# Four gate and up pairs of each swiglu FFN in seven half-size products, and the FFN's inner tiles in four groups

## Chip, cores, metric

The kernel runs on one core of a Trainium2 chip, in one launch. The metric is device time in microseconds, the median of several executions. Engines are named as the profile names them: PE is TensorE's matmul, PEld its weight load, DVE VectorE, ACT ScalarE, POOL GpSimd, and SP issues the weight loads from memory.

## What is computed

Two layers of a first block (FFN, mixer, FFN, gated embedding) and one layer of a second block, on 512 tokens of width 1024. The change touches only the swiglu FFNs of the first block, of which there are four (two layers, two FFNs each, hidden width 2816):

```python
def swiglu(x, w_gate, w_up, w_down):
    return (jax.nn.silu(x @ w_gate) * (x @ w_up)) @ w_down

for i in range(DEPTH):                      # DEPTH = 2
    h = rmsnorm(x, g_ffn1_pre[i])
    x = x + 0.5 * rmsnorm(swiglu(h, w1_gate[i], w1_up[i], w1_down[i]), g_ffn1_post[i])
    ...                                     # mixer: projections, two attentions, a convolution
    h = rmsnorm(x, g_ffn2_pre[i])
    x = x + 0.5 * rmsnorm(swiglu(h, w2_gate[i], w2_up[i], w2_down[i]), g_ffn2_post[i])
    ...                                     # gated embedding ("ple")
```

## The kernel before

Activations lie transposed: 128 features on the partitions, 512 tokens along the free axis. A tile is 128 x 512 in float32. Every product is done in three matmuls (`mm3`, L285 to L287): each operand is split into a high part, rounded to the fast float32 format, and a low part, the rest; the products high x high, low x high and high x low are added up in one PSUM bank, and low x low is left out. PSUM has eight banks of 128 x 512 in float32.

**Weights.** A unit is the weights of one output tile: for gate and up, 8 blocks of 128 x 128 (one for each 128 of the 1024 input features). SP loads units into `raw` tiles (L231); `prep` makes `wh` with a cast on ACT (L146) and puts the subtraction that makes `wl` on DVE (L147) into a list, which is flushed at the end of a step. `run` keeps `wu` units prepared ahead of the one in use.

**Order.** Nothing is rescheduled: each engine runs its instructions in the order in which the code of the steps issues them. A step is a matmul group or an evacuation; `later` holds what an evacuation postpones to the next step.

**A swiglu FFN** has 22 inner tiles n. For each, the gate product (8 x 3 matmuls of 512 columns into a bank `gu`) is multiplied on DVE by the token's norm factor `rb` into `gr` (L681) and put through Silu on ACT (L683); the up product likewise into `ur` (L706), then one step later `ur` is multiplied by `gr` (L712), and `split` makes `dh` on ACT (L306) and `dl` on DVE (L307). `pieces = (6, 8, 8)` groups the inner tiles: after each group the down products of that group run, 8 output tiles m, each summing over the group's tiles into a bank `pt`; they are added to `f` (copied on ACT for the first group, added on DVE, L779, for the others).

**The boundary** to the next stage is written out by hand in `PLAN`. The last four output tiles (m = 4 to 7) of the last group, the tail, are computed in two halves of 256 tokens, PA and PB. All four PA halves come first, then the PB halves, each cut in two (`mm_part`). Between the PB pieces stands the chain of the norm over PA: the sum of squares `acc` (L653 on ACT, L655 on POOL or DVE), a transpose on PE (`ss`, L314), a reduction on DVE (L315), the power on POOL (L323), a broadcast on PE (`bc`, L330), a copy on ACT (`sb`, L523), then for each of 8 feature tiles the update on DVE (L538, L539) and the new operand `hh` on ACT (L540), which the next stage's first products (`hd`, L638) read. Between the second FFN of a layer and the embedding stage eight small products (`pp`) stand between tail and head as well.

**The rope tables** (`rope_tables`, L403 to L447) are some thirty DVE instructions for the mixer's angles, hooked into the first FFN.

Of the kernel before, what the change touches and what calls it, by code (L numbers as in the profile page):

```python
# [21 lines left out]
N_ACT = 81  # L22
N_RAW = 4
RAW = 1024
WU_TAIL, WU_SB, WU_MLA = 10, 6, 6
N_TAIL = 4

# [41 lines left out]
class Column:  # L69


    def __init__(self, units, c):
        self.hi = lambda k: units[k].hi(0)[:, c]
        self.lo = lambda k: units[k].lo(0)[:, c]


class Raw:
# [18 lines left out]
class Builder:  # L96
# [31 lines left out]
    def cols_units(self, w, k0, kn, c0, ncol, width=P):  # L128
# [5 lines left out]

        return [Unit(lambda inp, c=c: host(inp, c), (kn, width)) for c in range(c0, c0 + ncol, width)]

    def prep(self, u):

        kn, w = u.dims
# [59 lines left out]
    def run(self):  # L199
# [7 lines left out]
                last[id(u)] = i  # L207
        raws = []
        for u in order:
            if len(raws) < 3 or raws[-1].n + u.n > RAW:  # L210
                raws.append(Raw())
            u.raw, u.at = raws[-1], raws[-1].n
            u.raw.units.append(u)
            u.raw.n += u.n
        for r in raws:
            r.left = sum(-(-u.dims[0] // (T // u.dims[1])) for u in r.units)
        self.declare(raws)
        frees = {}
        for u in order:
# [17 lines left out]
        def flush_low(us=None):  # L237
            keep = []
            for u, f in self.low:
                if us is None or u in us:  # L240
                    f()
                    u.raw.left -= 1
                    if u.raw.left == 0:
                        self.rlive -= 1
                else:
                    keep.append((u, f))
            self.low[:] = keep
            load_raws()

        def prep_next():  # L250
            u = order[self.uptr]
            if u.raw.tile is None:
                flush_low()
            assert u.raw.tile is not None
            self.prep(u)
            self.uptr += 1
            self.live += 1

        pos = {id(u): i for i, u in enumerate(order)}
        for m in range(3):  # L260
# [394 lines left out]
        eng.tensor_tensor(sub.acc[:, t0:t1], sub.acc[:, t0:t1], sq[:, t0:t1], op=ALU.add)  # L655


    def ffn(self, cols, pre, post, wg, wu, uoff, wd, pieces, pmul, padd, conv=None, nxt=None, first=False):
        V, S, G = self.V, self.S, self.G
        HT = sum(pieces)  # L660
        ahead = nxt.ahead if nxt else None
# [56 lines left out]
        def item(n, which):  # L718
            it = Sub()
            it.units = [gu[n] if which == 0 else uu[n]]  # L720

            def mm(p):
                pend[n, which] = self.ps("gu")
                self.mmk(pend[n, which], it.units[0], sub.h, p)

            def evac(p):
                (act_up if which else act_gate)(n, p, pend.pop((n, which)))

            it.mm, it.evac = mm, evac
            return it  # L730
# [8 lines left out]
            head = [Column(sub.by_k, slice(i * P, (i + 1) * P)) for i in range(4)]  # L739
        self.plain_head(sub, head, evac)  # L740

        def body():
            n0 = 0
            early = set()
            for pc, kn in enumerate(pieces):
                final = pc == len(pieces) - 1
# [2 lines left out]
                for n in range(max(n0, 2), n0 + kn, 2):  # L749
                    if final and ahead and n == n0 + kn - 4:  # L750
                        self.step(ahead[1])
                    if n not in early:
                        self.two(item(n, 0), item(n + 1, 0))
                    for i in (n, n + 1):
                        self.both(item(i, 1))
                if not final:
                    for i in (n0 + kn, n0 + kn + 1):
                        early.add(i)
                        self.both(item(i, 0))
                du = self.cols_units(wd, n0, kn, 0, D)  # L760
                for m in range(KD):
                    it = Sub()
# [1049 lines left out]
    def program(self):  # L1812
# [9 lines left out]
        for L in range(2):  # L1822
            ple = self.ple(L, colsA[L])
            c = colsA[L]
            seq.append(
                self.ffn(c, "g_ffn1_pre", "g_ffn1_post", mat("w1_gate", L), mat("w1_up", L), 0, mat("w1_down", L), (6, 8, 8), 4.0 / D, 4.0 * EPS, first=L == 0)
            )
            seq.append(self.mix1(L, c))
            seq.append(
                self.ffn(  # L1830
                    c, "g_ffn2_pre", "g_ffn2_post", mat("w2_gate", L), mat("w2_up", L), 0, mat("w2_down", L), (6, 8, 8), 4.0 / D, 4.0 * EPS, nxt=ple
                )
            )
            seq.append(ple)
# [46 lines left out]
def mat(name, L):  # L1881
    return lambda inp: inp[name][L]
# [28 lines left out]
```

## Time and profile before

| | us |
|---|---|
| median of 3 runs (2872.05 to 2875.48) | 2874.39 |
| the profiled execution | 2872.68 |
| its span, first to last instruction | 2870.8 |
| PE busy in the span | 2846.9 |
| DVE busy | 1706.1 |
| ACT busy | 1250.2 |

The span is what the views show; 1.9 us of the profiled execution lie around it. A matmul's end is modelled by the profile and runs over the start of the next one, so the pace of a row of matmuls is read from their starts, not from the duration of one.

### The profile page before, as it was taken

Reading aid. Unit: us, or ns where it says so; the run is one execution under the profiler, and the core shown is the slowest. Engines: PE = TensorE matmul, PEld = TensorE weight load, DVE = VectorE, ACT = ScalarE, POOL = GpSimd, SP = SyncE. Lnnn points to the kernel's source line nnn. Section 1 sums busy time; section 2 is a strip of 40 time slices with the busy share of each in tenths; the row PEclk is TensorE's granted clock in tenths of the full one; section 3 lists DMA queues with packets and bytes.
Section 4 is the critical chain, followed back from the end, with each engine's and each line's share of the span. In section 5 each row is a group of like instructions: output and inputs, shape, how many; then the busy total and the mean of one; then the engine's idle time right before and its main releaser. Section 6 shows DMA issues by size and latency. Waiting matters only on the chain.

```text
span 2870.8 us, 38496 instructions
## 1 busy us (share of the span) xinstructions
PE 2846.9 (99%) x14942; PEld 2445.0 (85%) x14946; DVE 1706.1 (59%) x3048; ACT 1250.2 (44%) x2464; POOL 217.3 (8%) x252
## 2 busy tenths in 40 slices
PE   9999999999999999999999999999999999999999
PEld 8888898798888998888987898888988889888888
DVE  6454476865434595434668674444788746735458
ACT  5342347653322464322457553323546635433234
POOL 0000110010000220000111100000300001000013
PEclk9999999999999999999999999999999999999999
DMA  5333311123223223222121223233222332322320
GB/s 180 113 103 96 101 64 53 52 82 118 96 96 110 74 77 122 100 91 100 64 83 56 85 74 115 91 103 103 76 81 92 103 103 84 115 96 96 110 96 30
DMA packets 77750, 264.30 MB, mean 92 GB/s; under 512 B 9088, under 2 KB 11008, under 8 KB 77568
## 3 DMA queue, kind: packets, MB, share of 16 engines
q1 hardware_dynamic: 75600, 259.29, 27.0%
q0 software_dynamic: 1536, 2.10, 0.3%
q8 instruction: 118, 1.93, 0.3%
q14 instruction: 64, 0.52, 0.1%
q10 hardware_dynamic: 432, 0.45, 0.0%
HBM read 257.61 MB, written 2.10 MB: 90 GB/s over the span
## 4 chain that ended last, share of the span: by engine, by line
PE 88%; DVE 7%; ACT 4%; issue 1%; DMA 0%; POOL 0%; SPq 0%; ACTq 0%; DVEq 0%
PE gu L286 13%; PE gu L287 13%; PE gu L285 13%; PE hd L638 9%; PE pt L286 8%; PE pt L287 8%; PE pt L285 8%; PE in L285 3%; PE in L286 3%; PE in L287 3%; ACT p L1392 1%; DVE wl L147 1%; DVE ptl L307 1%; DVE p L1401 1%; PE ro L285 1%
## 5 line engine op out<-in xcount | busy, mean ns | idle before, releaser
L147 DVE TENSOR_TENSOR wl<-raw,wh 128x512 fp32r<-128x512 f32 (+1 forms) x993 | 643.7, 693 | 147.7 <-ACT wh L146 143.7
L285 PE MATMUL gu<-hh,wh 128*128 128x512 f32 x1632 | 635.9, 390 | 0.0
L286 PE MATMUL gu<-hl,wh 128*128 128x512 f32 x1632 | 635.0, 389 | 0.0
L287 PE MATMUL gu<-hh,wl 128*128 128x512 f32 x1632 | 635.0, 389 | 0.0
L146 ACT CAST wh<-raw 128x512 fp32r<-128x512 f32 (+1 forms) x993 | 545.1, 605 | 200.0 <-PE pt L286 94.0
L285 PE MATMUL pt<-dh,wh 128*128 128x512 f32 (+1 forms) x1056 | 377.7, 358 | 0.0
L286 PE MATMUL pt<-dl,wh 128*128 128x512 f32 (+1 forms) x1056 | 376.9, 357 | 0.0
L287 PE MATMUL pt<-dh,wl 128*128 128x512 f32 (+1 forms) x1056 | 376.8, 357 | 0.0
L287 PEld LDWEIGHTS gu<-hh,wl 128*128 128x128 f32 x1632 | 306.3, 188 | 63.6
L285 PEld LDWEIGHTS gu<-hh,wh 128*128 128x128 f32 x1632 | 306.4, 188 | 63.4
L286 PEld LDWEIGHTS gu<-hl,wh 128*128 128x128 f32 x1632 | 306.4, 188 | 63.2
L306 ACT CAST dh<-ur 128x512 fp32r<-128x512 f32 x112 | 69.5, 621 | 462.8 <-DVE ur L712 462.8
L655 POOL TENSOR_TENSOR acc<-acc,sq 128x256 f32<-128x256 f32 (+1 forms) x96 | 100.5, 1046 | 1913.0 <-ACT sq L653 1912.3
L286 PEld LDWEIGHTS pt<-dl,wh 128*128 128x128 f32 x1056 | 199.5, 189 | 28.9
L285 PEld LDWEIGHTS pt<-dh,wh 128*128 128x128 f32 x1056 | 199.5, 189 | 28.9
L287 PEld LDWEIGHTS pt<-dh,wl 128*128 128x128 f32 x1056 | 199.5, 189 | 28.6
L706 DVE TENSOR_TENSOR ur<-gu,rb 128x512 f32<-128x512 f32 x102 | 70.4, 690 | 253.2 <-PE gu L287 253.2
L779 DVE TENSOR_TENSOR f<-pt,f 128x512 f32<-128x512 f32 (+1 forms) x100 | 58.4, 584 | 237.4 <-PE pt L287 237.3
L285 PE MATMUL in<-hh,wh 128*128 128x512 f32 x432 | 170.7, 395 | 3.0 <-DVE ptl L307 2.4
L638 PE MATMUL hd<-hh,wh 128*128 128x256 f32 (+1 forms) x672 | 169.8, 291 | 0.3 <-ACT hh L464 0.3
L287 PE MATMUL in<-hh,wl 128*128 128x512 f32 x432 | 168.4, 390 | 0.0
L286 PE MATMUL in<-hl,wh 128*128 128x512 f32 x432 | 168.3, 390 | 0.0
(396 smaller groups left out, 4439.8 us busy)
## 6 DMA issues: line engine op xcount, KB each, us to landing
raw<-in_w_dram SPq DMA_DIRECT2D x449, 512.0 KB, 3.3
raw<-in_w_dram SPq DMA_DIRECT2D x36, 384.0 KB, 3.0
x<-in_x_dram SPq DMA_DIRECT2D x8, 256.0 KB, 6.8
raw<-in_w_dram SPq DMA_DIRECT2D x4, 432.0 KB, 3.4
pt<-in_p_dram SPq DMA_DIRECT2D x6, 256.0 KB, 4.0
out_dram<-pgt SPq DMA_DIRECT2D x10, 128.0 KB, 1.7
qh<-qrh POOLq DMA_DIRECT2D x16, 64.0 KB, 2.1
ql<-qrl POOLq DMA_DIRECT2D x16, 64.0 KB, 2.3
```

The source lines that it names most:

```text
L146: self.S.copy(h, src)
L147: self.low.append((u, lambda h=h, l=l, src=src: self.V.tensor_sub(l, src, h.bitcast(F32))))
L285: self.E.matmul(o, lh, rh, start=start, stop=False, **kw)
L286: self.E.matmul(o, lh, rl, start=False, stop=False, **kw)
L287: self.E.matmul(o, ll, rh, start=False, stop=stop, **kw)
L306: self.S.copy(hi, src)
L307: self.V.tensor_sub(lo, src, hi.bitcast(F32))
L638: self.E.matmul(q, w, h, start=k == 0 and j == 0, stop=k == KD - 1 and j == 2)
L655: eng.tensor_tensor(sub.acc[:, t0:t1], sub.acc[:, t0:t1], sq[:, t0:t1], op=ALU.add)
L706: V.tensor_mul(ur[:, t0:t1], ou, sub.rb[:, t0:t1])
L779: V.tensor_tensor(f, q, f, op=ALU.add)
L1392: S.activation(s.p[t][:, c : c + n], s.sc[t][:, c : c + n], AF.Exp, bias=mx[qb], accum_out=s.sum[:, qb : qb + 1])
```

## The change

In each swiglu FFN the inner tiles n = 9, 11, 15 and 17 take the gate and up products by Strassen's identity. Gate and up weights of one tile are taken as one 2 x 2 matrix of blocks (gate and up, by lower and upper 512 input features) and the tokens as two halves A and B. Instead of 48 matmuls of 512 columns there are seven products of 4 x 3 matmuls of 256 columns, 84 in all, on sums of weight blocks (`part_sums`, tiles `q`) and sums of operand halves (`token_sums`, tiles `ts`, made once per FFN). Their results are put together on DVE and ACT out of two banks, `st.r` and `st.r3`; both halves of `st.r` are used. These tiles stand in turns with plain ones: the steps of tile 9 lie between those of 8, of 11 between those of 10, and so on. While they run, 5 units are prepared ahead instead of 8. The groups of inner tiles become (6, 6, 6, 4). The second block's FFN stays as it is.

```diff
-WU_TAIL, WU_SB, WU_MLA = 10, 6, 6
+WU_TAIL, WU_SB, WU_MLA, WU_SEVEN = 10, 6, 6, 5
+SEVEN = (9, 11, 15, 17)
...
+    def part_sums(self, u):
...
+        def add(key, a, b):
+            q[key] = self.a("q")
+            self.V.tensor_add(q[key], a, b)
+
+        if u.j == 0:
+            add("q1", w["21"], w["22"])
+        elif u.j == 1:
+            add("q2", q.pop("q1"), w["11"])
+        elif u.j == 2:
+            add("q4", q.pop("q2"), w["12"])
+            add("q3", w["11"], w["21"])
...
+        def token_sums(k):
+            g1, g2, x1, x2 = sub.gpre(k), sub.gpre(k + 4), self.X[k], self.X[k + 4]
+            xg, a, b = self.a("xg"), self.a("ta"), self.a("tb")
+            S.activation(xg, x1, AF.Copy, scale=g1)
+            V.tensor_sub(a[:, A], xg[:, A], xg[:, B])
+            V.scalar_tensor_tensor(a[:, B], x2[:, B], g2, xg[:, B], op0=ALU.mult, op1=ALU.subtract)
+            V.scalar_tensor_tensor(b[:, A], x2[:, B], g2, a[:, A], op0=ALU.mult, op1=ALU.add)
+            V.scalar_tensor_tensor(b[:, B], x2[:, A], g2, b[:, A], op0=ALU.mult, op1=ALU.subtract)
+            ah, al, bh, bl = (self.a("ts", F32R) for _ in range(4))
+            self.split(a, ah, al)
+            S.activation(bh, b, AF.Copy, scale=-1.0)
+            V.scalar_tensor_tensor(bl, b, -1.0, bh.bitcast(F32), op0=ALU.mult, op1=ALU.subtract)
...
+        def product(o, part, block, key, start):
+            h, l = part.blocks[block]
+            for k in range(4):
+                c = slice(k * P, (k + 1) * P)
+                self.mm3(o, h[:, c], l[:, c], *operand(key, k), start and k == 0, k == 3, skip=True)
...
+            def one():
+                st.r, st.r3 = self.ps("gu"), self.ps("gu")
+                product(st.r[:, A], u[0], "11", "11", True)
+                product(st.r[:, B], u[0], "q1", "t1", False)
+            def copy():
+                st.s = self.a("s15")
+                S.copy(st.s, st.r)
+            def two():
+                st.s2 = self.a("s2")
+                S.copy(st.s2[:, A], st.r[:, A])
+            def gate_a():
+                V.tensor_tensor(pair(n)[0][:, A], st.r3[:, A], st.s[:, A], op=ALU.add)
+            def gate_b():
+                gr = pair(n)[0]
+                V.tensor_tensor(gr[:, B], st.r[:, B], st.s2[:, A], op=ALU.add)
+                V.tensor_mul(gr, gr, sub.rb)
+                S.activation(gr, gr, AF.Silu)
+                self.later.append(lambda: V.tensor_mul(gr, gr, sub.rb))
+            def up_b():
+                V.scalar_tensor_tensor(pair(n)[1][:, B], st.r[:, A], -1.0, st.s[:, B], op0=ALU.mult, op1=ALU.subtract)
+            def out():
+                gr, ur = raw.pop(n)
+                V.scalar_tensor_tensor(ur[:, A], st.r[:, A], -1.0, gr[:, A], op0=ALU.mult, op1=ALU.mult)
+                V.tensor_mul(ur[:, B], ur[:, B], gr[:, B])
+                hid[n] = (self.a("dh", F32R), self.a("dl", F32R))
+                self.split(ur, *hid[n])
+            def last():
+                step(lambda: product(st.r[:, A], u[3], "22", "t4", False), [u[3]])
+                step(out)
+            step(one, [u[0]])
+            step(copy)
+            if prev:
+                prev()
+            self.both(item(m, 0))
+            step(lambda: product(st.r3[:, A], u[1], "12", "21", True), [u[1]])
+            step(gate_a)
+            step(lambda: product(st.r[:, A], u[1], "q2", "t2", False), [u[1]])
+            step(two)
+            self.both(item(m, 1))
+            step(lambda: product(st.r[:, A], u[2], "q3", "t3", False), [u[2]])
+            step(up_b)
+            step(lambda: product(st.r[:, B], u[2], "q4", "22", False), [u[2]])
+            step(gate_b)
+            return last
...
-mat("w1_down", L), (6, 8, 8), 4.0 / D, 4.0 * EPS, first=L == 0)
+mat("w1_down", L), (6, 6, 6, 4), 4.0 / D, 4.0 * EPS, first=L == 0, seven=SEVEN)
```

Three places in the order of instructions follow. In rows of the order a name with "waits" behind it waits for that engine's counter.

DVE before, in a plain pair of the first FFN: `ur<-gu` is the evacuation of an up product, `wl` a weight's low part, `dl` the low part of the finished inner tile.

```order
L706 TENSOR_TENSOR ur_1492<-gu_1503,rb_483 128x512
L147 TENSOR_TENSOR wl_1529<-raw_1366,wh_1528 128x512
L147 TENSOR_TENSOR wl_1532<-raw_1366,wh_1531 128x512
L712 TENSOR_TENSOR ur_1492<-ur_1492,gr_1491 128x512
L307 TENSOR_TENSOR dl_1535<-ur_1492,dh_1534 128x512
L706 TENSOR_TENSOR ur_1500<-gu_1544,rb_483 128x512
```

DVE now, at tile 17 of the first FFN (with 16 in turns): the same five, then `up_b`, which reads the left half of `st.r` (`gu_2347`).

```order
L775 TENSOR_TENSOR ur_2442<-gu_2487,rb_483 128x512
L200 TENSOR_TENSOR wl_2513<-raw_2383,wh_2512 128x512
L200 TENSOR_TENSOR wl_2516<-raw_2383,wh_2515 128x256
L781 TENSOR_TENSOR ur_2442<-ur_2442,gr_2441 128x512
L376 TENSOR_TENSOR dl_2519<-ur_2442,dh_2518 128x512
L890 SCALAR_TENSOR_TENSOR ur_2461<-gu_2347,s_493_2379 128x256
L884 TENSOR_TENSOR gr_2460<-gu_2347,s_514_2481 128x256
```

PE now, at the same place: the end of the product q3 into the left half of `gu_2347`, then the first matmul of the product q4, into the right half, with a wait on DVE's counter; before, the row of matmuls of the next product stood there without a wait.

```order
L354 MATMUL gu_2347<-ts_805,wh_2376 128x256
L355 MATMUL gu_2347<-ts_806,wh_2376 128x256
L356 MATMUL gu_2347<-ts_805,wl_2377 128x256
L354 MATMUL gu_2347<-hh_244,wh_2373 128x256 [waits DVE_49]
L355 MATMUL gu_2347<-hl_245,wh_2373 128x256
```

The value of the counter is that of `up_b`, in all 16 tiles of this kind.

ACT now, at tile 9 of the first FFN: `s<-gu` is the copy of `st.r`, which PE's fourth product (q2) waits for; it stands behind the two Sin of the rope tables, which wait for DVE.

```order
L514 ACTIVATE rope_s<-ang_1248 128x512 [waits DVE_49]
L515 ACTIVATE rope_c<-rc_1266 128x512 [waits DVE_49]
L375 CAST dh_1289<-ur_884 128x512 [waits DVE_49,PE_49]
L183 CAST wh_1321<-raw_1133 128x512 [waits DMAHW6_49]
L183 CAST wh_1324<-q_1242 128x512 [waits PE_49]
L872 COPY s_287_1327<-gu_1295 128x512 [waits PE_49]
```

Before, Silu and casts stood behind those two, and no copy of a bank that a product waits for.

PE now, in the first output tile of the last group of inner tiles: four groups of three matmuls, one for each inner tile 18 to 21; before there were eight, for 14 to 21.

```order
L354 MATMUL pt_3145<-dh_2951,wh_2948 128x512 [waits Activation_49]
L355 MATMUL pt_3145<-dl_2952,wh_2948 128x512 [waits DVE_49]
L356 MATMUL pt_3145<-dh_2951,wl_2949 128x512
L354 MATMUL pt_3145<-dh_2992,wh_2948 128x512 [waits Activation_49]
L355 MATMUL pt_3145<-dl_2993,wh_2948 128x512 [waits DVE_49]
L356 MATMUL pt_3145<-dh_2992,wl_2949 128x512
L354 MATMUL pt_3145<-dh_3101,wh_2948 128x512 [waits Activation_49]
L355 MATMUL pt_3145<-dl_3102,wh_2948 128x512 [waits DVE_49]
L356 MATMUL pt_3145<-dh_3101,wl_2949 128x512
L354 MATMUL pt_3145<-dh_3136,wh_2948 128x512 [waits Activation_49]
L355 MATMUL pt_3145<-dl_3137,wh_2948 128x512 [waits DVE_49]
```

The last group, of the inner tile finished last (21), now stands fourth instead of eighth.

## Rows read from the trace of the kernel before

**Rows 1.** The page: busy time of each engine; then the chain's shares by engine.

```profile
PE 2846.9 (99%) x14942; PEld 2445.0 (85%) x14946; DVE 1706.1 (59%) x3048; ACT 1250.2 (44%) x2464; POOL 217.3 (8%) x252
PE 88%; DVE 7%; ACT 4%; issue 1%; DMA 0%; POOL 0%; SPq 0%; ACTq 0%; DVEq 0%
```

**Rows 2.** Windows over the first FFN: busy time of each engine, clock, DMA share, GB/s.

```profile
59.00:343.00 284.00, 284.00 (x1255) 235.16 (x1254) 139.81 (x237) 92.84 (x168) 3.77 (x7) 1.00 0.32 102
```

**Rows 3.** Timeline of PE, plain gate products, 96 matmuls apart: start, duration, line.

```profile
59.65 0.39 PE L285 MATMUL gu<-hh,wh 128*128 128x512 f32 x1
...
81.41 0.39 PE L285 MATMUL gu<-hh,wh 128*128 128x512 f32 x1
```

**Rows 4.** Timeline of PE, tail in halves, 25 matmuls of 256 columns apart.

```profile
366.16 0.28 PE L285 MATMUL pt<-dh,wh 128*128 128x256 f32 x1
...
369.16 0.28 PE L286 MATMUL pt<-dl,wh 128*128 128x256 f32 x1
```

**Rows 5.** Timelines of PE, DVE and ACT behind an up product of the second FFN.

```profile
759.96 0.39 PE L285 MATMUL gu<-hh,wh 128*128 128x512 f32 x1
```

**Rows 6.** The same place on DVE: evacuation, weights, product, low part.

```profile
760.16 0.69 DVE L706 TENSOR_TENSOR ur<-gu,rb 128x512 f32<-128x512 f32 x1 [4.75 <-PE gu L287]
760.77 1.29 DVE L147 TENSOR_TENSOR wl<-raw,wh 128x512 fp32r<-128x512 f32 x2
761.97 0.69 DVE L712 TENSOR_TENSOR ur<-ur,gr 128x512 f32<-128x512 f32 x1
763.40 0.69 DVE L307 TENSOR_TENSOR dl<-ur,dh 128x512 fp32r<-128x512 f32 x1 [0.74 <-ACT dh L306]
```

**Rows 7.** The same place on ACT.

```profile
762.75 0.62 ACT L306 CAST dh<-ur 128x512 fp32r<-128x512 f32 x1 [5.64 <-DVE ur L712]
```

**Rows 8.** DVE behind an up product with no weights in between (first FFN).

```profile
123.09 0.69 DVE L706 TENSOR_TENSOR ur<-gu,rb 128x512 f32<-128x512 f32 x1 [3.01 <-PE gu L287]
...
125.19 0.69 DVE L307 TENSOR_TENSOR dl<-ur,dh 128x512 fp32r<-128x512 f32 x1 [0.69 <-ACT dh L306]
```

**Rows 9.** Groups by line and form, DVE: count, busy, mean ns.

```profile
L147 DVE TENSOR_TENSOR wl<-raw,wh 128x256 fp32r<-128x256 f32 x36 | 15.1, 420 | 0.0
```

**Rows 10.** Timelines in the mixer: DVE's low part, and PE, which waits for it.

```profile
576.44 0.69 DVE L307 TENSOR_TENSOR yl<-cv,yh 128x512 fp32r<-128x512 f32 x1
577.18 0.50 PE L286 MATMUL part<-yl,wh 128*128 128x512 f32 x1 [1.25 <-DVE yl L307]
```

**Rows 11.** Boundary behind the first FFN, PE: first PB piece, transpose, broadcast.

```profile
357.44 0.28 PE L285 MATMUL pt<-dh,wh 128*128 128x256 f32 x1
...
360.32 0.38 PE L314 MATMUL ss<-ident,acc 128*128 128x128 f32 x2
...
364.86 0.38 PE L330 MATMUL bc<-ident,s 128*128 128x128 f32 x2
```

**Rows 12.** The same boundary, DVE: sum of squares, weights, reduction, first update.

```profile
358.62 0.42 DVE L655 TENSOR_TENSOR acc<-acc,sq 128x256 f32<-128x256 f32 x1 [0.55 <-ACT sq L653]
...
360.87 1.28 DVE L147 TENSOR_TENSOR wl<-raw,wh 128x512 fp32r<-128x512 f32 x2
362.06 0.42 DVE L315 TENSOR_REDUCE ss<-ss 128x2 f32<-128x256 f32 x1
...
365.68 0.49 DVE L538 SCALAR_TENSOR_TENSOR t<-f,cols,sb 128x256 f32<-128x256 f32 x1 [0.43 <-ACT sb L523]
```

**Rows 13.** The same boundary: POOL's power.

```profile
362.86 0.71 POOL L323 TENSOR_TENSOR s<-ss,mhalf 128x2 f32<-128x2 f32 x1
```

**Rows 14.** ACT's operand of feature tile 5 there.

```profile
373.50 0.51 ACT L540 ACTIVATE hh<-x,cols 128x256 fp32r<-128x256 f32 x1 [1.77 <-DVE x L539]
```

**Rows 15.** DVE at the rope tables: the evacuation ahead, their start, what follows them.

```profile
128.53 0.69 DVE L706 TENSOR_TENSOR ur<-gu,rb 128x512 f32<-128x512 f32 x1 [1.44 <-PE gu L287]
...
134.03 0.43 DVE L410 CAST ang<-pos_i 128x512 f32<-128x512 int32 x1 [1.44 <-DMA pos_i<-in_positions_dram]
...
151.01 1.29 DVE L147 TENSOR_TENSOR wl<-raw,wh 128x512 fp32r<-128x512 f32 x2
```

More of the change, by code (lines that the diff above doesn't have):

```diff
@@ L74, in __init__, with blocks @@
         self.lo = lambda k: units[k].lo(0)[:, c]
+class Quad:
+    def __init__(self, hosts):
+        self.hosts, self.raws, self.q = hosts, None, {}
+        self.parts = [Part(self, j) for j in range(4)]
+    def blocks(self):
+        a, b = (r.tile for r in self.raws)
+        return {"22": a[:, 0:T], "11": a[:, T:], "12": b[:, 0:T], "21": b[:, T:]}
+class Part:
+    n, dims = 1024, (8, P)
+    def __init__(self, quad, j):
+        self.quad, self.j, self.blocks, self.summed = quad, j, {}, False
 class Raw:
@@ L209, in run @@
         for u in order:
+            if isinstance(u, Part):
+                if u.quad.raws is None:
+                    u.quad.raws = [Raw(), Raw()]
+                    for r, host in zip(u.quad.raws, u.quad.hosts):
+                        block = Unit(host, (8, P))
+                        block.at, r.units, r.n = 0, [block], RAW
+                    raws.extend(u.quad.raws)
+                u.raw = u.quad.raws[1]
+                continue
             if len(raws) < 3 or raws[-1].n + u.n > RAW:
@@ L216, in run @@
             r.left = sum(-(-u.dims[0] // (T // u.dims[1])) for u in r.units)
+        for u in order:
+            if isinstance(u, Part):
+                u.quad.raws[0].left, u.quad.raws[1].left = 7, 6
         self.declare(raws)
@@ L241, in flush_low @@
                     f()
[L242 to L244 removed]
+                    for r in (u.quad.raws[: 2 if u.j < 3 else 1] if isinstance(u, Part) else [u.raw]):
+                        r.left -= 1
+                        if r.left == 0:
+                            self.rlive -= 1
                 else:
@@ L257, in prep_next @@
             self.live += 1
+            nxt = order[self.uptr] if self.uptr < len(order) else None
+            if isinstance(nxt, Part) and all(r.tile is not None for r in nxt.quad.raws):
+                self.part_sums(nxt)
         pos = {id(u): i for i, u in enumerate(order)}
@@ L655, in final_sq, with ffn @@
         eng.tensor_tensor(sub.acc[:, t0:t1], sub.acc[:, t0:t1], sq[:, t0:t1], op=ALU.add)
-    def ffn(self, cols, pre, post, wg, wu, uoff, wd, pieces, pmul, padd, conv=None, nxt=None, first=False):
+    def ffn(self, cols, pre, post, wg, wu, uoff, wd, pieces, pmul, padd, conv=None, nxt=None, first=False, seven=()):
         V, S, G = self.V, self.S, self.G
@@ new lines, in operand @@
+        def operand(key, k):
+            if key in ("11", "21", "22"):
+                hh, hl = sub.h[k + 4 * (key[0] == "2")]
+                c = A if key[1] == "1" else B
+            else:
+                i = 0 if key in ("t1", "t3") else 2
+                hh, hl = sums[k][i : i + 2]
+                c = A if key in ("t1", "t2") else B
+            return hh[:, c], hl[:, c]
+        def product(o, part, block, key, start):
[3 more added lines that the diff above has]
+                self.mm3(o, h[:, c], l[:, c], *operand(key, k), start and k == 0, k == 3, skip=True)
@@ L742, in body @@
         def body():
-            n0 = 0
+            n0, left = 0, None
             early = set()
@@ L751, in body @@
                         self.step(ahead[1])
+                    if seven and n == 4:
+                        wu, self.wu = self.wu, WU_SEVEN
+                    if seven and n > seven[-1]:
+                        self.wu = wu
+                    if n + 1 in seven:
+                        left = seven_pair(n, n + 1, left)
+                        continue
                     if n not in early:
@@ L755, in body @@
                         self.both(item(i, 1))
+                        if seven and pc == 0:
+                            self.step(lambda k=i - 2: token_sums(k))
                 if not final:
```

41 lines of the change are left out of this document (39 added, 2 removed).

## The prediction

> **What bounds the kernel now.** I read the page first: PE is busy for 99% of the span and makes up 88% of the chain that ended last [rows 1]. Then the first FFN by itself: PE has work in all of its 284 us, at the full granted clock, while DVE is busy for 139.8 us of them, about half [rows 2]. So in the FFNs a matmul taken away is time gained, as long as PE does not start to wait for something; DVE and ACT cost nothing as long as they keep ahead. The reader is to see two things there: PE's pace, and how far DVE runs behind PE when it evacuates a bank. The pace: 96 matmuls of 512 columns take 81.41 - 59.65 = 21.76 us, 0.2267 each [rows 3]; 25 of 256 columns take 3.00 us, 0.1200 each [rows 4]. Half the columns cost 53%.
>
> **Gain 1, the seven products.** A plain gate and up pair is 48 x 0.2267 = 10.88 us; seven products are 84 x 0.1200 = 10.08 us. That is 0.80 us for a tile, 16 tiles: 12.8 us.
>
> The traced pace can be held against the Trainium skill, "TensorE: Matmul & The Clock Gate", section "Back-to-back issue gap": an isolated gap is N/2.4 + 2.5 ns at the warm clock, so 109 and 216 ns by estimate, and the gain would be 19.0 us instead of 12.8. The rows, with a weight load behind every matmul, are 11 ns slower for either width, and I stay with them.
>
> **Gain 2, the last group of four.** In the tail four output tiles use halves of 256 columns. Four inner tiles leave the last group, so 4 x 4 x 3 = 48 places per FFN take one matmul of 0.2267 instead of two of 0.1200: 0.64 us, four FFNs: 2.6 us. Gains together: 15.4 us.
>
> **Loss 1, the wait in front of q4.** This is the largest term. The order shows that PE's product q4 (right half of st.r) waits for `up_b`, DVE's read of the left half of the same bank. DVE runs its queue in order, and ahead of `up_b` stands everything that the plain neighbour's up product left: evacuation, one or two weights' low parts, the product with the gate, and `dl`, which itself waits for ACT. PE has only q3 to do meanwhile, 12 x 0.1200 = 1.44 us. How long DVE takes for this very chain stands in the trace. The next product's first matmul starts at 759.96 [rows 5], the evacuation at 760.16 and `dl` at 763.40 [rows 6], with ACT's cast between [rows 7]. A wide DVE instruction lets the next one start 0.61 later (760.16 to 760.77), so `up_b` starts 764.01 - 759.96 = 4.05 us after PE began q3. It is a half-wide instruction with two inputs, which takes 0.49 (the update) [rows 12], and PE follows DVE by 0.05 and loses 0.11 at the restart (576.44 + 0.69 to 577.18; first matmul 0.50 instead of 0.39) [rows 10]. The wait is 4.05 + 0.49 + 0.05 - 1.44 + 0.11 = 3.26 us. Tiles 9 and 15 have two full weights in the queue, tiles 11 and 17 one full and one of 256 columns (0.42 instead of 0.69 [rows 9]): 2.99 us. The very first tile has none, and then `dl` starts 2.10 instead of 3.24 behind the evacuation [rows 8]: 2.12 us. Sum: 7 x 3.26 + 8 x 2.99 + 2.12 = 48.8 us. No wait in a bank's other half is in the trace of before, so this is bounded: from above by the chain as timed (3.26), from below by DVE idle at that moment. Then `up_b` starts when q3's last matmul is done (1.32 + 0.28 [rows 4]) and the wait is 1.60 + 0.49 + 0.05 - 1.44 + 0.11 = 0.8 us, 13 us in all. I take the upper end, since the order puts the whole chain ahead of it. Below nothing is not possible.
>
> **Loss 2, the rope tables.** In the first FFN the tables' DVE work stands ahead of the evacuation of tile 7's up product, and ACT's copy of st.r for tile 9 stands behind that evacuation's cast. Counted from the evacuation of tile 6: before, the tables start 5.50 later (128.53 to 134.03) and take 16.98 (to 151.01) [rows 15]. After that, two weights 1.20, evacuation 0.61, product up to the cast 0.78 (761.97 to 762.75), four ACT instructions of 0.62 [rows 6, 7], release 0.05: 27.6. PE gets to q2 after 5.25 (24 x 0.2267, less the 0.20 between PE and DVE) + 2.88 + 5.44 + 1.44 = 15.0. It waits 12.6 us, 12.7 with the restart, once. Before, PE had only Silu evacuations behind the tables and free banks to go on with. Bounds: two casts now stand ahead of the tables' own loads, which can add 1.2; if the tables start earlier, up to 3 less.
>
> **Loss 3, the start of the last down products.** Inner tile 21, just finished, is needed after 9 matmuls (2.04 us) instead of 21 (4.76). With one weight in the queue its `dh` is there at 762.15 + 0.62 - 759.96 + 0.05 = 2.86, its `dl` at 3.58. PE waits 0.82 and, one matmul on, 0.38, each with a restart: 1.4 us, four FFNs: 5.7 us. Before, both came in time.
>
> **Loss 4, the boundary.** The PB pieces that cover the norm's chain are half as long. Let PE start them at 0 (357.44 [rows 11]). The sum of squares is done at 359.04 - 357.44 = 1.60 [rows 12]; before, PE asked for it at 2.88, now at 1.44: waits 0.21. The two transposes cost 0.22 (364.86 - 360.32 less 36 matmuls [rows 11]). On DVE an evacuation and two weights come next, so the reduction starts at 1.64 + 0.34 + 1.19 = 3.17 and the power is done 1.51 later (362.06 to 362.86 + 0.71 [rows 12, 13]); with the release 4.73. PE, three pieces on, is there at 4.03: waits 0.70. The first update starts 0.82 after the broadcast (364.86 to 365.68), the operand of feature tile 5 ends 8.33 after that (373.50 + 0.51 [rows 14]): 13.9. PE is there at 4.73 + 0.22 + 2.16 + 5 x 0.96 + 0.22 = 12.1: waits 1.8. With three restarts 3.0 us. This holds behind a layer's first FFN. Behind the second, eight `pp` products (48 x 0.12 = 5.8 us) lie between, the last wait goes, and PE may wait instead for ACT to empty their banks: 1.1 + 0.5, from 1.1 to 2.9. Two of each: 9.2 us, from 5 to 13.
>
> **What I cost at nothing.** Token sums, four weight sums a tile, the copies and eight more additions to `f` per FFN. For a tile and its plain neighbour DVE has about 22 wide instructions (13.4 us) and five half ones (2.1) in PE's 21.0 us plus the wait. PE's matmuls cover them, since five units are ready ahead; were the cover gone, each wide one would cost PE 0.6 us. Loads move as many weights as before, with DMA at a third of its time [rows 2].
>
> **Sum.** 48.8 + 12.7 + 5.7 + 9.2 = 76.4 us lost, 15.4 gained: 61.0 slower. From the profiled execution's 2872.7 (1.7 under the median, no more than runs differ) that is **2934 us**, 2.1% slower. Its own range is 2920 to 2946.
>
> **Rivals.** *A: DVE is free when `up_b` is due.* If the neighbour's chain is over within 1.6 us, loss 1 is 13 us and the time 2898. For it: DVE has idle time in the FFN (half). Against: the chain starts only when the neighbour's product ends, whatever DVE did before, and took 3.24 us to `dl` [rows 6].
>
> *B: halves of a bank do not bind each other.* Then loss 1 is nothing, losses 2 to 4 stay, and the time is 2872.7 - 15.4 + 27.6 = 2885. Against: the wait stands in the order, 16 times.
>
> The Trainium skill, "PSUM — Partial Sum Buffer", section "PSUM bank collisions raise a hardware error", says to guard a bank by semaphores, not an address in it: another half collides as well. By that rule B falls and the wait is needed; no run shown here has such a pair.
>
> *C: DVE is late nowhere, and the kernel is faster.* All four losses have one root, DVE's queue behind a product that just ended. If it costs PE nothing, the arithmetic alone counts: 2857. It decides at the point where the losses shrink to a fifth (15.4 of 76.4). For it: PE waits for DVE in no FFN before. Against: there eight banks lie between PE and the evacuation; here PE asks for the same bank 1.44 us later.
>
> *D: the delay spreads.* If, besides `up_b`, the last product waits a whole product's time (1.44 us) for the gate's half or a weight, 16 x 1.44 = 23 us more: 2957. Against: 2.88 us of products lie between them.
>
> **Chances.** Forecast 0.75, A 0.08, B 0.05, C 0.05, D 0.07. The range, 2896 to 2948, takes in the forecast, A and the low part of D. Times within 0.2% (5.7 us) can hardly be told from no change; no case ends there, 0.01 is left for it. Faster 0.05, slower 0.94.
>
> **What would show it.** In the profile after: matmuls of 256 columns in `gu` at 0.12 us; PE idle ahead of q4 with DVE `ur` L890 as releaser, 16 times, near 3 us; once some 12 us ahead of q2 with ACT `s15`; four waits each of `pt` for `dh` and `dl`; `ss`, `bc` and `hd` waiting at the boundaries. I am wrong if PE's idle time for L890 is under 20 us, if the pace of 256 columns in `gu` is not 0.12, or if the clock falls under 1.00 in the FFNs.

## The result, and the profile after

| | before | after |
|---|---|---|
| median, us | 2873.2 (4 runs, 2872.1 to 2875.5) | 2950.6 (4 runs, 2950.2 to 2953.0) |
| ratio | | 1.0269 [1.0256, 1.0283] |
| profiled execution, us | 2872.7 | 2950.7 |
| PE idle in the span, us | 23.9 | 91.8 |

The changed kernel is 2.7% slower. The prediction was 2934, from 2896 to 2948: the direction and the main cause were right, but 17 us of the loss had no place in the sum, and the time lies 2.6 us above the range. All "what is missing" below is counted on the profiled executions: 78.0 us measured, 61.0 predicted.

The page of the changed kernel: busy times by engine, then the shares of the chain that ended last.

```profile
PE 2857.1 (97%) x15326; PEld 2465.1 (84%) x15330; DVE 1863.8 (63%) x3384; ACT 1324.5 (45%) x2624; POOL 217.2 (7%) x252
...
PE 82%; DVE 11%; ACT 4%; issue 2%; DMA 0%; POOL 0%; ACTq 0%; SPq 0%; DVEq 0%; POOLq 0%
```

Against [rows 1], DVE has gained share in the chain (7 to 11%) and PE lost it (88 to 82%). Two things are to be seen in the first line. PE stands idle for 68 us more than before, which is what the prediction said it would do (76 us, of which restarts count as busy). But PE is also busy for 10.2 us more (2846.9 before), though the change takes some 15 us of matmuls away: about 25 us of PE's own time were not expected. A restart and the modelled end of the last matmul ahead of a wait cost 0.26 each (0.27 at 512 columns) and count as busy; with 37 new waits they explain about 10 us. The rest needs another cause.

Who PE waited for in all (engine, line, releaser: us in total, times, longest):

```profile
PE gu L354 <- DVE ur L890: 42.6, 16, 2.9
PE gu L354 <- ACT s L872: 11.9, 1, 11.9
PE ss L383 <- DVE acc L724: 6.4, 4, 1.6
...
PE pt L354 <- ACT dh L375: 2.6, 4, 0.7
...
PE bc L399 <- POOL s L392: 2.1, 6, 0.4
...
PE hd L707 <- ACT hh L609: 1.6, 2, 0.8
...
PE pt L355 <- DVE dl L376: 0.9, 4, 0.2
```

Every wait of the prediction is there: 16 in front of q4, one in front of q2, four and four at the last group, and those at the boundaries. Those at the boundaries have other sizes: PE waits 1.6 us for `acc` at each, where 0.21 was predicted; for `bc` it waits less (0.36 instead of 0.70) and for `hd` too (0.8 instead of 1.8).

One wait in front of q4, from PE's and DVE's timeline (start, duration, engine, line, operation, in brackets the idle time before it and its releaser):

```profile
791.02 0.28 PE L354 MATMUL gu<-ts,wh 128*128 128x256 f32 x1
...
795.48 0.39 PE L354 MATMUL gu<-hh,wh 128*128 128x256 f32 x1 [2.87 <-DVE ur L890]
```

```profile
791.22 0.69 DVE L775 TENSOR_TENSOR ur<-gu,rb 128x512 f32<-128x512 f32 x1 [4.68 <-PE gu L356]
791.83 0.68 DVE L184 TENSOR_TENSOR wl<-raw,wh 128x512 fp32r<-128x512 f32 x1
792.43 0.69 DVE L184 TENSOR_TENSOR wl<-q,wh 128x512 fp32r<-128x512 f32 x1
793.03 0.68 DVE L781 TENSOR_TENSOR ur<-ur,gr 128x512 f32<-128x512 f32 x1
794.40 0.69 DVE L376 TENSOR_TENSOR dl<-ur,dh 128x512 fp32r<-128x512 f32 x1 [0.68 <-ACT dh L375]
795.01 0.42 DVE L890 SCALAR_TENSOR_TENSOR ur<-gu,s 128x256 f32<-128x256 f32 x1
```

This is the chain that the prediction put together from [rows 5 to 7], link by link: q3 starts at 791.02, `up_b` at 795.01, 3.99 later (4.05 predicted). DVE had been idle for 4.68 us before the neighbour's product ended; it is late only because its queue starts there.

Now the busy time. PE in stretches around two waits of the same kind and nearly the same length (stretch: its length, busy us and instructions of PE, PEld, DVE, ACT, POOL, then the granted clock, DMA's share and GB/s):

```profile
1864.00:1866.00 2.00, 0.00 (x0) 0.00 (x0) 1.32 (x3) 1.08 (x3) 0.00 (x0) 0.99 0.00 0
...
1868.00:1870.00 2.00, 2.00 (x11) 2.00 (x11) 0.38 (x1) 0.00 (x0) 0.00 (x0) 0.50 0.59 152
...
1971.00:1973.00 2.00, 0.00 (x0) 0.00 (x0) 1.32 (x3) 1.45 (x3) 0.00 (x0) 1.00 0.00 0
...
1975.00:1977.00 2.00, 2.00 (x19) 2.00 (x19) 1.94 (x4) 0.79 (x2) 0.00 (x0) 1.00 0.66 207
```

Behind the first wait the granted clock is 0.50 (1.2 GHz), and PE has 11 matmuls in 2 us; behind the second it stays at 1.00 (2.4 GHz), with 19. The pace at 0.50, from two matmuls of 256 columns that lie 22 apart:

```profile
1867.24 0.42 PE L356 MATMUL gu<-hh,wl 128*128 128x256 f32 x1
...
1871.94 0.41 PE L354 MATMUL gu<-ts,wh 128*128 128x256 f32 x1
```

That is 0.214 each, against 0.120 at 1.00 [rows 4]; 512 columns take 0.427, against 0.227. Before the change the clock was 1.00 in the FFN [rows 2] and in every stretch but the last few us of the program. In the profile after it falls behind seven waits:

```profile
150.01:156.00 5.99, 5.99 (x20) 5.30 (x21) 4.13 (x9) 4.62 (x9) 0.00 (x0) 0.51 0.45 115
186.92:190.00 3.08, 3.08 (x13) 3.06 (x14) 0.11 (x1) 0.00 (x0) 0.00 (x0) 0.50 0.06 25
606.30:610.00 3.70, 3.70 (x9) 2.93 (x10) 1.47 (x3) 0.02 (x1) 0.00 (x0) 0.54 0.34 124
1234.14:1238.00 3.86, 3.86 (x19) 3.86 (x20) 2.28 (x5) 0.00 (x0) 0.00 (x0) 0.56 0.39 134
1677.46:1682.00 4.54, 4.54 (x13) 3.59 (x14) 1.47 (x3) 0.03 (x1) 0.00 (x0) 0.62 0.29 110
1866.65:1874.00 7.35, 7.35 (x39) 7.35 (x40) 5.27 (x9) 1.72 (x4) 0.00 (x0) 0.58 0.38 110
1893.18:1898.00 4.82, 4.82 (x20) 4.42 (x21) 1.87 (x4) 0.72 (x2) 0.00 (x0) 0.65 0.04 12
```

Each stretch begins with the first matmul after a wait, and PE is busy throughout. What the clock took is the distance from each matmul to the next, less its pace at 1.00 and less the restart (0.11): 2.7 + 1.4 + 1.6 + 1.5 + 1.6 + 2.7 + 1.5, 12.9 us before rounding. The first stands behind the rope tables' wait, four behind waits for L890 (7.0 us together), and two (3.2 us) in the mixers, behind waits for `yl` that were there before the change as well [rows 10] and cost no clock then.

So the theory to be tested is: (T) the waits of the prediction, plus a clock that falls behind some of them (12.9 us), plus a boundary that was sized too small. Its rivals: the waits only cover a DVE that has too much to do; or the clock falls for a reason that has nothing to do with the waits.

### The profile page after: what moved, and what is told of

It reads as the page before. It is cut to its first block, busy times and chain, and to the rows that moved or that the text cites. A ratio compares the mean times of both kernels' runs of the same rounds, so it can differ in the third digit from the quotient of the medians.

```text
span 2948.9 us, 39730 instructions
## 1 busy us (share of the span) xinstructions
PE 2857.1 (97%) x15326; PEld 2465.1 (84%) x15330; DVE 1863.8 (63%) x3384; ACT 1324.5 (45%) x2624; POOL 217.2 (7%) x252
## 4 chain that ended last, share of the span: by engine, by line
PE 82%; DVE 11%; ACT 4%; issue 2%; DMA 0%; POOL 0%; ACTq 0%; SPq 0%; DVEq 0%; POOLq 0%
PE gu L354 12%; PE gu L355 12%; PE gu L356 12%; PE hd L707 8%; PE pt L355 8%; PE pt L356 8%; PE pt L354 8%; PE in L354 3%; PE in L355 3%; PE in L356 3%; DVE wl L200 2%; ACT p L1581 1%; DVE ptl L376 1%; DVE p L1590 1%; PE ro L354 0%
## 5 line engine op out<-in xcount | busy, mean ns | idle before, releaser
L200 DVE TENSOR_TENSOR wl<-raw,wh 128x512 fp32r<-128x512 f32 (+1 forms) x961 | 606.9, 674 | 121.5 <-ACT wh L199 117.2
L354 PE MATMUL gu<-hh,wh 128*128 128x512 f32 (+1 forms) x1568 | 596.9, 381 | 42.6 <-DVE ur L890 42.6
L199 ACT CAST wh<-raw 128x512 fp32r<-128x512 f32 (+1 forms) x961 | 515.5, 590 | 193.8 <-DMA raw<-in_w_dram 121.3
L355 PE MATMUL gu<-hl,wh 128*128 128x512 f32 (+1 forms) x1568 | 593.9, 379 | 0.0
L356 PE MATMUL gu<-hh,wl 128*128 128x512 f32 (+1 forms) x1568 | 593.1, 378 | 0.0
L356 PE MATMUL pt<-dh,wl 128*128 128x512 f32 (+1 forms) x992 | 365.6, 369 | 0.0
L356 PEld LDWEIGHTS gu<-hh,wl 128*128 128x128 f32 x1568 | 298.5, 190 | 54.4
L354 PEld LDWEIGHTS pt<-dh,wh 128*128 128x128 f32 x992 | 187.0, 188 | 35.6 <-ACT dh L375 4.3
L355 PEld LDWEIGHTS pt<-dl,wh 128*128 128x128 f32 x992 | 187.0, 188 | 33.6 <-DVE dl L376 2.2
L356 PEld LDWEIGHTS pt<-dh,wl 128*128 128x128 f32 x992 | 186.9, 188 | 30.9
L968 DVE TENSOR_TENSOR f<-pt,f 128x512 f32<-128x512 f32 (+1 forms) x132 | 79.6, 607 | 203.4 <-PE pt L356 203.4
```

Of the source, the lines that this page charges most:

```text
L354: self.E.matmul(o, lh, rh, start=start, stop=False, **kw)
L355: self.E.matmul(o, lh, rl, start=False, stop=False, **kw)
L356: self.E.matmul(o, ll, rh, start=False, stop=stop, **kw)
L968: V.tensor_tensor(f, q, f, op=ALU.add)
```

## Experiments

### A bank of its own for the right half

```diff
-                st.r, st.r3 = self.ps("gu"), self.ps("gu")
+                st.r, st.rb, st.r3 = self.ps("gu"), self.ps("gu"), self.ps("gu")
...
-                product(st.r[:, B], u[0], "q1", "t1", False)
+                product(st.rb[:, B], u[0], "q1", "t1", True)
...
-            step(lambda: product(st.r[:, B], u[2], "q4", "22", False), [u[2]])
+            step(lambda: product(st.rb[:, B], u[2], "q4", "22", False), [u[2]])
```

(The copy of both halves and `gate_b` read `st.rb` accordingly.)

> The changed kernel, but the right half of st.r (q1*t1, then q4) has a PSUM bank of its own, so that q4 no longer shares a bank with what up_b reads. T (PE waits for DVE's queue only because of the shared bank, and the granted clock falls to its lower level, 0.50, behind some of these waits): PE's idle time for L890 was 42.6 us in 16 waits, with 0.26 more for each at the modelled end and the restart 46.8 us, and the stretches at clock 0.50 behind four of them cost 7.6 us; both go: 2950.6 - 54.4 = 2896, from 2889 to 2904 (the stretches behind other waits may come and go). Rival, the delay only moves on (DVE gets to gate_b or to the next weights' low parts as late, and PE waits there instead): less than half of it comes back, 2923 or more. Rival, the clock falls for another reason (its low stretches stay though the waits go): 2904.

Measured: 2893.4 us, 1.0072 [1.0057, 1.0087] of before: 57.2 us come back, T's 54.4 and 2.8 more. The group of matmuls that had waited 42.6 us (line, engine, operation, tiles, count; busy us, mean ns; idle before them):

```profile
L354 PE MATMUL gu<-hh,wh 128*128 128x512 f32 (+1 forms) x1568 | 591.6, 377 | 0.0
```

No wait took its place. DVE still runs every instruction it ran before, so it was never short of time, only asked too early; the prediction's rival D (the delay spreads) falls for good. And of the seven stretches at clock 0.50 only the rope tables' remains (2.4 us): four went with the waits for L890, and the two in the mixers went too, although the waits there stayed at 1.26. By the rows, 46.8 us of waits, 7.0 of clock behind them and 3.2 in the mixers make 57.0.

### The rope tables later

```diff
+                    if first and pc == 2 and m == 7:
+                        self.rope_at = len(self.steps)
...
-                self.hook(60, [self.setup_late, lambda: None, lambda: None, self.rope_tables, lambda: None, self.lam])
+                self.hook(self.rope_at, [self.rope_tables])
+                self.hook(60, [self.setup_late, lambda: None, lambda: None, lambda: None, lambda: None, self.lam])
```

> The changed kernel, but the rope tables' DVE work stands behind the last down product but one of the third group, some 200 us later, where eight PSUM banks lie between PE and DVE. T: the wait of 11.90 us in front of the first q2 goes, with 0.26 at the end and the restart, and so does the stretch at clock 0.50 behind it (2.9 us): 2950.6 - 15.1 = 2935.5, from 2931 to 2939. Rival, the first tile waits for its own loads and sums just as long: 2948 to 2951. Rival, the tables cost PE as much in their new place (weights' low parts behind them): 2945 or more, with PE's wait for a wl near 330 us.

Measured: 2938.7 us (2936.0 to 2940.8), 1.0229 [1.0214, 1.0244]: 11.9 us back, within T's bounds and 3 short of its middle. The wait of 11.9 us for L872 and the low clock behind it are gone, and nothing waits at the tables' new place. What is short is the clock again. In this execution it falls behind nine waits, seven of the 16 for L890 and the two in the mixers, and takes 14.5 us, where 10.2 would be left of the 12.9 without the tables' stretch. One of them, with a wait of 2.87, behind which it had stayed at 1.00 in the profile after:

```profile
885.07:892.00 6.93, 6.93 (x45) 6.93 (x46) 5.28 (x9) 2.48 (x5) 0.00 (x0) 0.75 0.42 135
```

So whether the clock falls behind a wait does not follow from the wait's length alone.

### Work in the wait

```diff
+            def idle_fill():
+                o, h = self.ps("gu"), u[2].blocks["q3"][0]
+                for i in range(20):
+                    self.E.matmul(o[:, A], h[:, 0:P], operand("t3", 0)[0], start=True, stop=True)
...
             step(up_b)
+            step(idle_fill, [u[2]])
```

> The changed kernel, with twenty more matmuls of 256 columns (2.4 us) into a bank that nobody reads, between q3 and q4 of every tile: PE works where it stood idle, DVE's queue is as before. T (the low clock follows from PE's idle time in front of q4): a wait of 2.6 to 2.9 us becomes 2.4 us of work and a wait of 0.2 to 0.6; the time up to q4 is the same, but the four stretches at clock 0.50 behind L890 (7.6 us) go: 2943, from 2939 to 2946. Rival, the low clock has nothing to do with the idle time: 2950, with low stretches behind q4 as before. Rival, the wait isn't DVE's but counts from PE's own work: 16 x 2.4 = 38 us more, 2989.

Measured: 2942.1 us, 1.0240 [1.0223, 1.0257]: 8.5 us faster, by doing 320 matmuls more. The wait for L890, and the stretch behind which the clock had fallen at 1866:

```profile
PE gu L354 <- DVE ur L890: 4.9, 15, 0.5
```

```profile
1864.00:1868.00 4.00, 3.81 (x31) 3.81 (x32) 3.37 (x7) 1.00 (x3) 0.00 (x0) 1.00 0.37 116
1868.00:1872.00 4.00, 4.00 (x28) 3.67 (x27) 3.15 (x7) 3.36 (x7) 0.00 (x0) 1.00 0.38 114
```

Counted from the evacuation ahead of it on DVE, q4 starts when it started before in 15 of the 16 tiles (3.99 or 4.26 later), and 0.45 later in the very first, whose wait had been 1.79; what is gained is clock alone. None of the 16 is followed by a low clock now; those behind the tables and in the mixers are as in the profile after. That settles it for these four stretches: the clock falls there because PE stands idle in front of q4. They had cost 7.0 us by the rows; the 8.5 between the medians agrees with that within the 3 us that executions of either kernel differ by.

### The groups alone

The kernel before, with this one change (twice):

```diff
-... mat("w1_down", L), (6, 8, 8), 4.0 / D, ...
+... mat("w1_down", L), (6, 6, 6, 4), 4.0 / D, ...
```

> The kernel before, with its inner tiles in groups of 6, 6, 6 and 4, and no seven products. T (losses 3 and 4 come from the short last group alone): pt's waits 1.4 x 4 = 5.7 us, and at the four boundaries what the changed kernel showed, 3.5 us behind a first FFN and 1.8 behind a second, 10.7 us; the tail's 192 places give back 2.6: 2873.2 + 13.8 = 2887, up to 2891 where the clock falls behind some wait. Rival, they come from the seven products that stand ahead of the last group (DVE late from there): 2870.6. Forecast's own terms: 2873.2 + 5.7 + 9.2 - 2.6 = 2885.5.

Measured: 2893.6 us, 1.0072 [1.0057, 1.0087]: 20.6 us slower than before, more than T's 13.8 (and above its upper bound, 2891) and than the forecast's 12.3. The short last group costs this without any seven products. The same four places in the timeline, of the kernel before and then of this one (the first of before is in [rows 10]):

```profile
1030.60 0.39 PE L285 MATMUL pp<-ph,wh 128*128 128x256 f32 x1 [1.22 <-ACT prj L865]
1618.00 0.50 PE L286 MATMUL part<-yl,wh 128*128 128x512 f32 x1 [1.27 <-DVE yl L307]
2071.76 0.39 PE L285 MATMUL pp<-ph,wh 128*128 128x256 f32 x1 [1.18 <-ACT prj L865]
```

```profile
582.84 0.50 PE L286 MATMUL part<-yl,wh 128*128 128x512 f32 x1 [1.26 <-DVE yl L307]
1041.82 0.39 PE L285 MATMUL pp<-ph,wh 128*128 128x256 f32 x1 [1.24 <-ACT prj L865]
1634.38 0.50 PE L286 MATMUL part<-yl,wh 128*128 128x512 f32 x1 [1.26 <-DVE yl L307]
2094.01 0.39 PE L285 MATMUL pp<-ph,wh 128*128 128x256 f32 x1 [1.20 <-ACT prj L865]
```

They lie 5.66, 11.22, 16.38 and 22.25 us later. 3.2 us of that is a low clock behind the two `yl` rows and 0.35 a longer wait behind the second of them. The four FFNs so cost 5.7, 4.0, 5.2 and 3.9 us, 18.7 in all; with gain 2 added (2.6) and loss 3 taken off (5.6, whose waits are 0.65 and 0.22 here too) the boundary is 15.6 us where 9.2 was predicted. DVE and POOL in front of the wait for `acc` show why (the third of DVE's four low parts, which the first row merges, stands below it by itself):

```profile
359.61 3.59 DVE L147 TENSOR_TENSOR wl<-raw,wh 128x512 fp32r<-128x512 f32 x4
...
360.90 1.70 DVE L147 TENSOR_TENSOR wl<-raw,wh 128x512 fp32r<-128x512 f32 x1
...
363.12 0.41 DVE L779 TENSOR_TENSOR f<-pt,f 128x256 f32<-128x256 f32 x1
...
360.50 1.55 POOL L655 TENSOR_TENSOR acc<-acc,sq 128x512 f32<-128x512 f32 x1 [1.18 <-ACT sq L653]
...
364.13 1.20 POOL L655 TENSOR_TENSOR acc<-acc,sq 128x256 f32<-128x256 f32 x1 [2.08 <-ACT sq L653]
...
367.29 0.42 DVE L655 TENSOR_TENSOR acc<-acc,sq 128x256 f32<-128x256 f32 x1 [1.56 <-POOL acc L655]
```

PE ended the tail's first piece at 360.23, but DVE evacuated it at 363.12: four low parts of the next weights stood ahead of it. Three of them took 0.68 or 0.69 each; the third began while POOL was adding (360.50 to 362.05) and took 1.70, so 1.0 of the 2.9 us is that one. ACT's squares and POOL's additions follow from there, and the sum is done at 367.71, 3.2 us after PE began the PB pieces (358.80 + 48 x 0.12), not 1.6. The next two runs ask which of the two is at fault.

### DVE in place of POOL

```diff
-                            self.final_sq(sub, f, p, last, m == 0)
+                            self.final_sq(sub, f, p, True, m == 0)
```

> The kernel before in groups of 6, 6, 6 and 4 again (groups_only), but the sum of squares of the FFN's output is added up by DVE throughout, not by POOL in all places but the last. In groups_only the sum for the first half was done 1.78 us after PE asked for it, behind POOL's additions of 1.20 and 0.77 us each that now come every 1.44 us. T (POOL's chain of additions is what PE waits for at the boundary): the sum is done with ACT's last square and one addition, some 0.6 to 1.1 us earlier, four times: 2893.6 - 2.4 to 4.4 = 2889 to 2891, and PE's wait for acc falls under 1.2. Rival (DVE's evacuation stands behind four weights' low parts, and POOL only follows): 2893 to 2896, the wait for acc stays at 1.5 or more.

(On the kernel with the groups alone.) Measured: 2913.4 us, 1.0140 [1.0126, 1.0154], 20 us slower than the groups alone. Neither reason foresaw that. PE's wait for `acc` grows from 1.6 to 4.6 us each, and a low clock follows each (6.4 us together):

```profile
PE ss L314 <- DVE acc L655: 18.3, 4, 4.6
```

```profile
367.92 0.42 DVE L779 TENSOR_TENSOR f<-pt,f 128x256 f32<-128x256 f32 x1
368.82 0.42 DVE L655 TENSOR_TENSOR acc<-acc,sq 128x256 f32<-128x256 f32 x1 [0.48 <-ACT sq L653]
369.16 0.42 DVE L779 TENSOR_TENSOR f<-pt,f 128x256 f32<-128x256 f32 x1
370.06 0.42 DVE L655 TENSOR_TENSOR acc<-acc,sq 128x256 f32<-128x256 f32 x1 [0.48 <-ACT sq L653]
```

DVE's queue is in order: each addition waits there for ACT's square (about 0.5 idle each time), and the next piece's evacuation waits behind the addition, so the pieces follow each other every 1.24 us, though PE's last matmul ahead of the wait had begun at 365.63. POOL's slow additions had kept that dependence off DVE's queue. On the question it was made for the run gives one row only: with POOL not adding, the four low parts ahead of the first evacuation took 2.49 us (from 361.76) instead of 3.59.

### Fewer weights ahead at the boundary

```diff
-        wu, self.wu = self.wu, WU_TAIL
+        wu, self.wu = self.wu, 8 if prev.pmul == 4.0 / D and not hasattr(nxt, "ahead") else WU_TAIL
```

> The kernel before in groups of 6, 6, 6 and 4 (groups_only), but at the two boundaries behind a layer's first FFN eight units of weights are made ready ahead instead of ten, so that DVE has two low parts instead of four in a row in front of the first evacuation of the tail. T (PE waits for acc at the boundary because DVE evacuates late behind the next weights' low parts, and ACT's squares and POOL's additions follow): at these two boundaries the first evacuation of a 256-column piece comes within 1.3 us of PE's last matmul of it (2.9 in groups_only) and PE's wait for acc falls from 1.62 to under 0.7; it stays 1.56 at the two others. 2893.6 - 2 to 4 = 2890 to 2892. Rival (POOL's additions, 1.20 and 0.77 us each, one for 1.44 us of PE, are the limit by themselves): the waits for acc stay above 1.2, 2893.

(On the kernel with the groups alone.) Measured: 2888.9 us, 1.0053 [1.0038, 1.0068], 4.7 us less than the groups alone and a little under T's 2890 to 2892. Between the two profiled executions 1.6 us is a stretch of low clock that did not come. The evacuation comes 0.57 us after PE's piece (359.76) and the wait for `acc` is gone from the list at the two places that were changed; at the two others it is what it was:

```profile
359.13 1.28 DVE L147 TENSOR_TENSOR wl<-raw,wh 128x512 fp32r<-128x512 f32 x2
360.33 0.42 DVE L779 TENSOR_TENSOR f<-pt,f 128x256 f32<-128x256 f32 x1
```

```profile
PE ss L314 <- DVE acc L655: 3.1, 2, 1.6
```

POOL still adds, at 0.74 for a piece, and keeps up. It is the burst of low parts that makes the boundary late: work for the next stage, made ready at a rate of one unit a step, in steps that have become half as long. The low part that POOL had slowed went with the burst; no run tells the two apart, and the boundaries behind a layer's second FFN were left as they were.

### The three sources undone together

The separate bank, the tables behind the second group's first down product, and the groups back at (6, 8, 8) with tiles 9, 11, 17 and 19. What stays is the seven products.

> The changed kernel with the three sources of waiting undone together: q1*t1 and q4 in a bank of their own, the rope tables behind the second group's first down product, and the groups back at 6, 8, 8 (tiles 9, 11, 17 and 19 in seven products). What is left of the change is gain 1 alone. T (DVE and ACT keep up when nobody waits for them in order): 2873.0 - 12.8 = 2860, from 2856 to 2865, no wait for L890, L872 or the last group's dh. By sums from own_bank: 2893.4 less the tables' 15.1 and the groups' 17 to 20.6 gives 2858 to 2861. Rival, the extra DVE and ACT work (some 2 us of DVE more in a tile) costs PE in other places once the large waits no longer hide it: 2866 to 2880, with new waits of gu for weights' low parts or for ur. Rival, gain 1 is smaller than 0.80 a tile: between 2865 and 2873 with no new wait.

Measured: 2861.7 us (five runs, 2861.1 to 2862.0), 0.9960 [0.9946, 0.9973] of before: faster than the kernel before by 11 us, and than the changed one by 89. Its page, the busy times and the chain's shares:

```profile
PE 2836.7 (99%) x15522; PEld 2463.0 (86%) x15522; DVE 1835.8 (64%) x3320; ACT 1319.3 (46%) x2608; POOL 217.4 (8%) x252
...
PE 88%; DVE 7%; ACT 3%; issue 1%; DMA 0%; POOL 0%; SPq 0%; ACTq 0%; DVEq 0%
```

No wait of PE is listed in the FFNs, the chain's shares are those of before within one point of a hundred, and the clock is 1.00 up to the last us or two. The time lies within T's 2856 to 2865. Gain 1 is real: 11.1 us instead of 12.8, 0.69 a tile. DVE's 130 us of extra work brought PE no wait.

### A fifth tile

```diff
-SEVEN = (9, 11, 17, 19)
+SEVEN = (9, 11, 13, 17, 19)
```

> As three_undone, with tile 13 in seven products too: 20 tiles instead of 16. T (a tile in seven products is worth 0.80 us as long as PE waits for nothing): 2861.7 - 4 x 0.80 = 2858.5, from 2857 to 2860. Rival (DVE's and ACT's extra work has no room left, three tiles in a row): PE waits in gu, 2862 or more.

Measured: 2859.9 us (2857.5 to 2860.5), 0.9952 [0.9939, 0.9964]; 1.9 us less than four tiles, with no wait in `gu` and, in the profiled execution, one stretch of low clock that cost 1.5 us, behind a `yl` wait. It is just within T's 2857 to 2860 and the fastest of all kernels here by its median, though its distance from the last one is less than its own runs differ by (3.1 us).

## Why the prediction was right and wrong

Its terms, in us, with where the measure is from:

| term | predicted | measured | from |
|---|---|---|---|
| loss 1, wait in front of q4 | 48.8 (its addends give 48.9) | 46.8 | 42.6 + 16 x 0.26 |
| loss 2, rope tables | 12.7 | 12.2 | 11.9 + 0.26 |
| loss 3, last down products | 5.7 | 5.6 | 4 x (0.65 + 0.22 + 2 x 0.27) |
| loss 4, boundary | 9.2 | 15.6 | the groups alone |
| clock | 0 | 12.9 | seven stretches |
| gain 1 | -12.8 | -11.1 | three sources undone |
| gain 2 | -2.6 | (-2.6) | taken as predicted |
| sum | 61.0 | 79.4 | 78.0 in the profiled execution |

The terms overshoot the whole by 1.4 us, less than one stretch of low clock, which comes or goes between executions.

**Losses 1 to 3 were right**, in place, number and size. They were worked out as a chain of DVE's queue from an ordinary tile, and the separate bank and the later tables, taken away one at a time, gave back what they should. The 2 us by which loss 1 is too large are two small readings: the chain took 3.99 instead of 4.05, and `up_b` 0.42, where the update's 0.49 had been taken for it. Rivals A, B and D fall: DVE was idle before the chain (4.68 us), and late all the same; the wait for the shared bank holds PE all 16 times; the delay doesn't spread. (No run keeps the shared bank without that wait, so whether the chip needs it stays untested.)

**What failed first: no term for the clock.** The prediction took the pace of [rows 3, 4] at clock 1.00 as given behind every wait, and listed a clock under 1.00 only among the things that would make it wrong. The trace of before had PE waits of 1.25 us [rows 10], but none near 2.9, so it showed what a wait costs only where the clock stayed. The clock took 12.9 us, most of the 17 that were missing. The sum should have had a second price for each long wait, from nothing to about the wait's cost again, and a range to match; with loss 4 alone put right the forecast would have been 2940, still 10 us short.

**What failed second: loss 4, 9.2 instead of 15.6.** Step "the sum of squares is done at 1.60" took DVE's evacuation of the PA pieces from a tail in which PE took 2.88 us for each [rows 12], and only halved the time PE gave it. It didn't count what else falls into that shorter time: the next stage's low parts, prepared by step and not by time. The evacuation was 2.9 us late, 1.0 of it by the one low part that ran beside POOL, and PE waited 1.6 us for `acc` four times, not 0.21. The later waits (`bc` 0.36, `hd` 0.82) were smaller than predicted (0.70, 1.8), since PE itself came later. Behind a layer's second FFN the prediction put 1.6 us, for which it shows no row, on ACT's emptying of the `pp` banks; that wait did not grow (1.22 and 1.18 before, 1.18 and 1.19 after), and what PE waited for there was `acc` again.

**Gain 1 was a little too large** (12.8, measured 11.1; the ratio's interval makes it 8 to 16 us), which is no difference that the runs can show. The pace in `gu` was the predicted one, 0.12 a matmul of 256 columns. The 19.0 us that the Trainium skill's "Back-to-back issue gap" ("TensorE: Matmul & The Clock Gate") gave by estimate lie outside that interval: the traced pace decides.

**Rival C, the gain alone,** was judged rightly: the three sources of waiting had to be taken away before the arithmetic showed. It is what the kernel with all three undone does.

What stays open: behind which wait the clock falls. Waits of 2.60 to 2.87 us were followed by 0.50 in four cases of 15 in the profile after, and waits of 2.47 to 2.87 in seven of 16 with the tables later, three of them at the same places; the four of 4.5 to 4.6 us with DVE in place of POOL all were. The mixers' waits for `yl`, 1.25 to 1.27 in all kernels, were followed by it in the changed kernel and with the groups alone, and not before, with the separate bank or with all three undone. It was not tried to place a wait on purpose.

## What to carry to other kernels

Where a bank is shared by two half-wide results, ask what stands in the reading engine's queue between the first half's last product and its reader; here that queue, not the engine's load, set the wait, and a second bank took it away whole. Price a new PE wait of some us twice: the wait, and, as here, up to as much again (2.7 us behind 2.9) for the half clock that may follow it; filling such a wait with matmuls that nobody needs was faster than leaving it empty. And where a stage is cut into shorter steps, count the work that is handed out by step (weights made ready, low parts): it stays as it was while the time to do it shrinks.

## Not expected of the hardware

The granted clock fell to 0.50 behind a single wait of 2.86 us (at 1234.14) after 150 us of PE work at 1.00 with no wait longer than 0.4, and behind a pair of waits of 0.49 and 1.26 with one matmul between them (at 606.30 in the profile after). It came back by itself, after 1.4 to 2.7 us of lost time, while PE was working.

A low part of 512 columns on DVE takes 0.68 us, and sometimes up to 1.7. In the trace of before, all 28 of them (of 953) that took over 1 us had begun during an instruction of POOL; 35 others that had begun so took under 0.75.
